# A decoder step on one core: where the rows' factors are spread, and how far the gating unit's loads stand ahead of their readers

## The chip, the core and the metric

The kernel runs on one core of one Trainium2 chip. The core has a matrix engine (PE; its weight loads are listed apart as PEld), a vector engine (DVE), a scalar engine for functions and copies (ACT), a general engine (POOL) and a sequencer that mostly issues transfers (SP). Each engine has its own queue and works through it in order; what an engine reads from another is guarded by semaphores. The metric is the device time of one execution in microseconds (us), smaller is better. One execution is also profiled; its times are read from the span's start.

## What is computed

The reference is one step of a decoder layer for a prompt (1024 rows of width 1024) and for eight sample rows that attend to a paged cache of 8192 positions. Cut to what matters here:

```python
def mixer_inputs(xn, w_in, b_f, g_sgu_v):          # xn = rmsnorm(x, g_mix)
    h = xn @ w_in                                  # columns: q | k | v | f | u | z
    q, k, v = ...
    logf = log_sigmoid(h[f] + b_f)
    u = gelu(h[u]);  z = rmsnorm(gelu(h[z]), g_sgu_v)

def sgu_prompt(u, z, w_s, b_s):                    # the gating unit, chunks of 128 rows
    mixed = einsum('hts,bcshd->bcthd', tril(w_s), z in chunks) + b_s
    return u * mixed

xp = xp + concat(rmsnorm(attention(q, k, v, logf)), rmsnorm(sgu_prompt(u, z))) @ w_o
xp = xp + cross_attend(rmsnorm(xp), memory)        # 4 heads, 256 memory tokens
xp = xp + conv_ffn(rmsnorm(xp))                    # width 2816, causal convolution of width 3
```

The sample rows pass through the same layer, with their keys and values gathered from the cache. RMSNorm of the input is not applied to x before the projection: the kernel multiplies the gain into x, multiplies by the weights, and applies each row's factor (one over the root mean square) when it takes the product out.

## The kernel before, in words

**Products.** Every float product with a weight is made of three matmuls on operands split in a high and a low part (`wh`/`wl` for weights, `xh`/`xl` for activations): high by high, high by low, low by high. Weights come in as `wr` (four buffers), ACT makes the high part (line 213) and DVE or POOL the low part (line 214), in four `wl` and five `wh` buffers. Large activation tiles share 18 buffers with the tag `u`; 512-column scratch tiles share seven with the tag `t2` (shown as `t`). PSUM tiles for products take `ba` (four) or `bb` (two) in turn by a counter (`BK`), every third one `bb`.

**Stages of the prompt.** `p1` makes q, f/u, k, v and z. Then come `attention(0)` for the first 512 rows with `fill` mixed in (the memory's keys and values, `pmem`, and then `gating(0)`, the first unit), `attention(1)`, and for each half of 512 rows: merge, output product, cross-attention, feed-forward. `gating(1)`, the second unit, is mixed into the first half's cross-attention.

**The start of p1.** `loaded(O_Q, ...)` brings x transposed (`load_x`, lines 216 and 217 split it) and the weights of q in four groups, each with the sample rows' small products (line 260). `stats(hf)` loads 512 rows of x as rows, sums their squares on ACT (line 205), and takes the root on DVE and POOL (lines 198, 199). The same function then spreads the four column factors along the free axis: DVE writes a 128x512 tile with them on diagonals (line 342), PE multiplies it by ones (line 349), and ACT copies the result into `rrow` (line 350). Both calls of `stats` and the sample's sum (`sample_sum`, lines 272 and 274) stand ahead of the queries' products: `by_cols(0)` runs 96 matmuls of four accumulators, with the four groups of weights as the outer loop (lines 423 to 425), `mm_cols(1, ...)` another 96 (lines 248 to 250). `evac_T` takes each of the eight results out with `rrow` (line 408) and splits it (lines 213, 214).

**The gating unit.** `gating(hf)` loads the gain (`gsv`, line 592) and the mixing weights (line 594, masked by DVE in line 595), and then for two pairs of 128-row chunks loads `z` and `u` (lines 602, 603), scales z (line 605, DVE), multiplies (line 613, PE) and combines (line 623, DVE). At the end it scales by the rows' factors and stores (lines 640, 641).

**The order.** All stages are generators. A `yield d` hands over control and tells how much work was just written, in units near 1 us of matmuls. `mix(main, bg, ratio)` lets the background generator take one step whenever the sum of the main one's units times the ratio exceeds what the background has used. The same units pace the sample rows' work, which is a generator of 148 steps of cache reading (`decode`; a K step multiplies on DVE or POOL in line 1205 and sums in line 1209, a V step multiplies on PE in line 1264) and then 87 smaller steps (`sample_rest`, of which the last groups read `w_down`): one step for each 7.5 units in p1, 20 in the first attention, 15 in the second, 6.0 in the middle stages, 7.5 and 8 in the feed-forward stages, 4.0 once the cache is done. Steps that are left when the prompt has ended are written behind it.

```python
def fill():
    yield from pmem()
    yield from gating(0)
att = yield from mix(att0, fill0, 1.0)
...
sq = yield from mix(cross(xt, sq), gating(1), 0.05)
```

What is written is a priority, not yet an order: a planner walks through the program with estimated durations and puts each engine's instructions in the order in which they become ready by its estimate, earlier written ones first. Buffers of one tag are handed out in the order in which their tiles are written.

Of the kernel before, what the change touches and what calls it, by code (L numbers as in the profile page):

```python
# [80 lines left out]
def build(nc, tc, ctx, a, phases=None):  # L81
# [13 lines left out]
    def nm(s):  # L95
        cnt[0] += 1
        return f"{s}_{cnt[0]}"

    def U(shape, dt=F32):
        n = 1  # L100
        for s in shape[1:]:
            n *= s
        t = upool.tile([P, UW], dt, tag="u", bufs=NU, name=nm("u"))[:, :n]
        if len(shape) == 3:
            t = t.rearrange("p (a b) -> p a b", b=shape[2])
        return t

    def T2(n=512, dt=F32):
        return tpool.tile([P, 520], dt, tag="t2", bufs=NT, name=nm("t2"))[:, :n]

    def KV():
        return dpool.tile([P, 2048], F32, tag="kv", bufs=NKV, name=nm("kv"))

    def sm(shape, tag, bufs=2, dt=F32):
        return small.tile(shape, dt, tag=tag, bufs=bufs, name=nm(tag))
# [9 lines left out]
    def BK():  # L125
        turn_[0] += 1
        return BB() if turn_[0] % BR == BR - 1 else BA()
# [66 lines left out]
    def rstd_of(ssq, n, width, tag):  # L194

        p = ssq.shape[0]
        r = sm([P, width], tag + "r", 2)[:p]
        nc.vector.tensor_scalar(r, ssq, 1.0 / n, EPS, op0=ALU.mult, op1=ALU.add)
        nc.gpsimd.tensor_tensor(r, r, mhalf[:p, :width], op=ALU.pow)
        return r  # L200

    def ssq_into(dst, src):
        n = src.shape[-1]
        j = tpool.tile([P, 1024], BF16, tag="junk", bufs=1, name=nm("junk"))[: src.shape[0], :n]
        nc.scalar.activation(j, src, AF.Square, accum_out=dst)
# [38 lines left out]
    def gemm3(out, pairs):  # L244

        n = len(pairs)
        for i, (sh, sl, mh, ml) in enumerate(pairs):
            mmul(out, sh, mh, start=(i == 0), stop=False)  # L248
            mmul(out, sh, ml, start=False, stop=False)  # L249
            mmul(out, sl, mh, start=False, stop=(i == n - 1))  # L250
# [57 lines left out]
    def p1(early):  # L308
        rstd = const.tile([P, 8], F32, tag="rstd", name="rstd")
# [19 lines left out]
        def stats(hf):  # L329
            for q in range(2):  # L330
                xr = KV().rearrange("p (c d) -> p c d", d=D)
                t0 = hf * 4 + q * 2
                with tc.issue_after(x_in):
                    nc.sync.dma_start(xr, a["x"][t0 * P : (t0 + 2) * P, :].rearrange("(c p) d -> p c d", p=P))
                for i in range(2):
                    ssq_into(ssx[:, t0 + i : t0 + i + 1], xr[:, i, :])
            c = slice(hf * 4, hf * 4 + 4)
            r = rstd_of(ssx[:, c], D, 4, "r4")
            nc.vector.tensor_copy(rstd[:, c], r)

            dg = T2()
            nc.vector.tensor_tensor(
                dg.rearrange("p (i t) -> p i t", t=P),
                ident.unsqueeze(1).broadcast_to((P, 4, P)),
                r.unsqueeze(2).broadcast_to((P, 4, P)),
                op=ALU.mult,
            )
            ps = BK()
            mmul(ps, ones, dg, start=True, stop=True)
            nc.scalar.activation(rrow[:, hf, :], ps, AF.Copy)  # L350
# [52 lines left out]
        def evac_T(ps, hf, hp, scale, hi, lo, out=None):  # L403

            c = slice(hf * 512, hf * 512 + 512)
            rows = slice(hp * P, (hp + 1) * P)
            t, h, l = T2(), T2(512, F32R), T2(512, F32R)
            nc.vector.scalar_tensor_tensor(t, ps, scale, rrow[:, hf, :], op0=ALU.mult, op1=ALU.mult)  # L408
            split(t, h, l)
            nc.scalar.dma_start(hi[rows, c], h.bitcast(F32))  # L410
            nc.scalar.dma_start(lo[rows, c], l.bitcast(F32))
            if out is not None:
                nc.sync.dma_start(out[rows, c], t)

        def by_cols(hf, ws):

            pss = [BK() for _ in range(4)]
            c = slice(hf * 512, hf * 512 + 512)
            for k in range(8):
                wh, wl = ws[k // 2][0][:, k % 2, :], ws[k // 2][1][:, k % 2, :]  # L420
                for i in range(4):
                    cb = slice(i * P, (i + 1) * P)
                    mmul(pss[i], wh[:, cb], xh[k][:, c], start=(k == 0), stop=False)
                    mmul(pss[i], wh[:, cb], xl[k][:, c], start=False, stop=False)
                    mmul(pss[i], wl[:, cb], xh[k][:, c], start=False, stop=(k == 7))
                yield 2.6
            return pss
# [14 lines left out]
        def mm_cols(hf, hp, ws, out):  # L442
            c, cb = slice(hf * 512, hf * 512 + 512), slice(hp * P, (hp + 1) * P)
            gemm3(
                out,
                [(ws[k // 2][0][:, k % 2, cb], ws[k // 2][1][:, k % 2, cb], xh[k][:, c], xl[k][:, c]) for k in range(8)],
            )

        pss = yield from by_cols(0, ws)
        for i in range(8):  # L450
            ps = BK() if i > 3 else pss[i]
            if i > 3:
                mm_cols(1, i - 4, ws, ps)
                yield 5.2
            evac_T(ps, i // 4, i % 4, 0.125, qh_d, ql_d)

# [91 lines left out]
        for tt in range(8):  # L548
            if tt < 4:
                ps = BK()  # L550
                mm_chunk(tt, ws, ps, 0, 512)
                if tt == SD:
# [5 lines left out]
                    r = rstd_of(ssv, AW, 1, "r1")  # L558
# [12 lines left out]
                    r = rstd_of(ssv, AW, 1, "r1")  # L571
# [12 lines left out]
        r = rstd_of(ssz, AW, 8, "r8")  # L584
# [5 lines left out]
    def gating(hf):  # L590
        gsv = T2()
        nc.sync.dma_start(gsv, a["g_sgu_v"].broadcast_to((P, 512)))
        wst = U([P, 8, P])
        nc.sync.dma_start(wst, a["wsT"])
        nc.vector.tensor_tensor(wst, wst, tri.unsqueeze(1).broadcast_to((P, 8, P)), op=ALU.mult)
        us_, ssu = [], sm([P, 4], "ssu", 1)
        for pr_ in range(2):
            z = U([P, 2, 512])
            u = U([P, 2, 512])
            t0 = hf * 4 + pr_ * 2  # L600
            rows = slice(t0 * P, (t0 + 2) * P)
            nc.sync.dma_start(z, zg_d[rows, :].rearrange("(c p) d -> p c d", p=P))
            nc.sync.dma_start(u, sgu_d[rows, :].rearrange("(c p) d -> p c d", p=P))
            for i in range(2):
                nc.vector.scalar_tensor_tensor(
                    z[:, i, :], z[:, i, :], rz[:, t0 + i : t0 + i + 1], gsv, op0=ALU.mult, op1=ALU.mult
                )
            yield 1
            for q in range(2):
                ps = BK()  # L610
                for j in range(4):
                    h = q * 4 + j
                    mmul(
                        ps[:, j * P : (j + 1) * P].rearrange("p (c d) -> p c d", d=64),
                        wst[:, h, :],
                        z[:, :, h * 64 : (h + 1) * 64],
                        start=True,
                        stop=True,
                    )
                for j in range(4):  # L620
                    h = q * 4 + j
                    uh = u[:, :, h * 64 : (h + 1) * 64]
                    nc.vector.scalar_tensor_tensor(
                        uh,
                        ps[:, j * P : (j + 1) * P].rearrange("p (c d) -> p c d", d=64),
                        gp[:, B_S + h : B_S + h + 1],
                        uh,
                        op0=ALU.add,
                        op1=ALU.mult,
                    )  # L630
                yield 1
            for i in range(2):
                ssq_into(ssu[:, pr_ * 2 + i : pr_ * 2 + i + 1], u[:, i, :])
            us_.append(u)
        r = rstd_of(ssu, AW, 4, "r4")
        for pr_ in range(2):
            u = us_[pr_]
            t0 = hf * 4 + pr_ * 2
            for i in range(2):
                nc.vector.tensor_scalar(u[:, i, :], u[:, i, :], r[:, pr_ * 2 + i : pr_ * 2 + i + 1], None, op0=ALU.mult)  # L640
            nc.sync.dma_start(sgn_d[t0 * P : (t0 + 2) * P, :].rearrange("(c p) d -> p c d", p=P), u)
        yield 1
# [950 lines left out]
    def prompt():  # L1593
        def fill():
            yield from pmem()
            if not G0R:
                yield from gating(0)
# [5 lines left out]
        def early():  # L1603
            next(att0)
            next(fill0)

        yield from p1(early)
        phase[0] = "att0"
        att = yield from mix(att0, fill0, MIXR)
# [150 lines left out]
```

## Time and profile before

| | |
|---|---|
| three runs | 2012.66 us median (2010.02 to 2018.85) |
| the profiled execution | 2016.49 us, of which the span from first to last instruction is 2014.7 us |
| PE busy | 1831.1 us, 91% of the span |
| DVE busy | 1329.0 us, 66% |
| ACT busy | 699.8 us, 35% |
| POOL busy | 976.4 us, 48% |
| mean granted PE clock | 0.963 |
| moved by DMA | 533.83 MB, 265 GB/s |

A row of the timeline gives the start, the length, the engine, the line, the operation, output and inputs, the shape, the count of merged instructions, and in brackets how long the engine had been idle before it and what ended that idle time. SPq rows are transfers issued by SP. A row of the windows view gives for a stretch of time each engine's busy time with its count (PE, PEld, DVE, ACT, POOL), then the granted PE clock, the DMA share and GB/s. Matmuls overlap, so a matmul's length is larger than the distance to the next one.

### The profile page before, as it was taken

The numbers are of one execution on the slowest core, as the hardware profiler recorded it, in microseconds if no ns is written. First come the engines' busy times: TensorE is split into PE (matmuls) and PEld (weight loads), VectorE is DVE, ScalarE is ACT, GpSimd is POOL, SyncE is SP. The second block draws the span as 40 slices with busy tenths as digits, with TensorE's granted clock in tenths as the row PEclk, the third lists the DMA queues.
The fourth block names the chain that finished last, engine by engine and source line by source line (L and its number), as shares of the span: only waits on it lengthen the run. The fifth ranks groups of instructions, "written<-read, shape, count | busy, mean of one in ns | idle before, by whom it ended". The sixth has DMA issues, their size and how long they took to land.

```text
span 2014.7 us, 24057 instructions
## 1 busy us (share of the span) xinstructions
PE 1831.1 (91%) x9083; PEld 1291.1 (64%) x9083; DVE 1329.0 (66%) x1456; ACT 699.8 (35%) x1284; POOL 976.4 (48%) x543
## 2 busy tenths in 40 slices
PE   3999997959998997989889998998899999899996
PEld 1797765646676655667657676676466767567772
DVE  4757766557646799998997999967524428633232
ACT  5132234436732423422322332333324433242431
POOL 1442464323267757667657675567243344232420
PEclk9999998979998998999989999999898999999999
DMA  9566799878696888788778697978755358666665
GB/s 340 189 230 209 275 325 324 262 213 236 219 355 238 316 316 326 270 316 331 275 257 338 248 330 296 373 290 322 294 185 199 119 178 278 241 196 221 251 229 189
DMA packets 161107, 533.83 MB, mean 265 GB/s; under 512 B 21832, under 2 KB 33352, under 8 KB 128224
## 3 DMA queue, kind: packets, MB, share of 16 engines
q0 software_dynamic: 38528, 270.88, 36.2%
q1 hardware_dynamic: 113248, 244.64, 35.8%
q10 hardware_dynamic: 9216, 16.78, 2.2%
q8 instruction: 71, 1.16, 0.2%
q14 instruction: 44, 0.36, 0.0%
HBM read 504.12 MB, written 28.13 MB: 264 GB/s over the span
## 4 chain that ended last, share of the span: by engine, by line
PE 59%; DVE 19%; DMA 10%; issue 5%; POOL 3%; ACT 2%; SPq 0%; POOLq 0%; DVEq 0%; ACTq 0%
PE ba L248 10%; PE ba L250 9%; PE ba L249 9%; PE bb L248 5%; PE bb L249 5%; PE bb L250 5%; DVE kv L1205 4%; PE dv L1264 3%; DVE s L1209 3%; DMA kv<-cache_k,kidx 3%; POOL wl L214 2%; DMA wr<-w_o 2%; DVE u L214 2%; PE dv L1507 1%; DVE t L1083 1%
## 5 line engine op out<-in xcount | busy, mean ns | idle before, releaser
L214 POOL TENSOR_TENSOR wl<-wr,wh 128x1024 fp32r<-128x1024 f32 (+1 forms) x184 | 458.0, 2499 | 331.7 <-PE ba L250 210.7
L213 ACT ACTIVATE wh<-wr 128x1024 fp32r<-128x1024 f32 (+2 forms) x220 | 228.1, 1042 | 327.5 <-PE ba L249 78.4
L1205 DVE TENSOR_TENSOR kv<-kv,d 128x2048 f32<-128x2048 f32 (+1 forms) x108 | 290.1, 2690 | 56.9 <-DMA kv<-cache_k,kidx 49.2
L1197 POOL DMA_INDIRECT kv<-cache_k,kidx x128 | 165.2, 1291 | 312.8 <-DVE s L1209 165.8
L1209 DVE TENSOR_REDUCE s<-kv 128x32 f32<-128x2048 f32 (+1 forms) x137 | 291.9, 2136 | 33.0 <-POOL kv L1205 32.0
L1258 POOL DMA_INDIRECT kv<-cache_v,kidx x128 | 179.6, 1403 | 182.4 <-PE dv L1264 69.6
L248 PE MATMUL ba<-wh,u 128*128 128x512 f32 (+1 forms) x612 | 239.8, 394 | 10.8 <-ACT u L213 6.3
L248 PE MATMUL ba<-u,wh 128*128 128x512 f32 x616 | 247.7, 403 | 0.0
L250 PE MATMUL ba<-u,wl 128*128 128x512 f32 x616 | 244.9, 398 | 0.0
L249 PE MATMUL ba<-u,wh 128*128 128x512 f32 x616 | 244.2, 397 | 0.0
L249 PE MATMUL ba<-wl,u 128*128 128x512 f32 (+1 forms) x612 | 236.9, 388 | 6.8 <-DVE wl L214 5.3
L250 PE MATMUL ba<-wh,u 128*128 128x512 f32 (+1 forms) x612 | 235.4, 387 | 6.8 <-DVE u L214 6.8
L1205 POOL TENSOR_TENSOR kv<-kv,d 128x2048 f32<-128x2048 f32 (+1 forms) x29 | 121.8, 4205 | 86.1 <-DMA kv<-cache_k,kidx 74.0
L1264 PE MATMUL dv<-kv,s 128*32 128x512 f32 x1024 | 139.9, 627 | 15.5 <-DMA kv<-cache_v,kidx 14.1
L248 PEld LDWEIGHTS ba<-wh,u 128*128 128x128 f32 x612 | 118.7, 194 | 53.7 <-issue 18.0
L248 PEld LDWEIGHTS ba<-u,wh 128*128 128x128 f32 x616 | 117.1, 190 | 47.6 <-issue 15.9
L250 PEld LDWEIGHTS ba<-wh,u 128*128 128x128 f32 x612 | 118.1, 193 | 40.0 <-DVE u L214 9.3
L249 PEld LDWEIGHTS ba<-wl,u 128*128 128x128 f32 x612 | 118.6, 194 | 36.0 <-DVE wl L214 5.9
L250 PEld LDWEIGHTS ba<-u,wl 128*128 128x128 f32 x616 | 116.6, 189 | 33.3 <-issue 7.3
L249 PEld LDWEIGHTS ba<-u,wh 128*128 128x128 f32 x616 | 116.9, 190 | 32.6 <-issue 6.8
L248 PE MATMUL bb<-u,wh 128*128 128x512 f32 x312 | 125.6, 402 | 2.1 <-DVE t L408 2.1
L249 PE MATMUL bb<-u,wh 128*128 128x512 f32 x312 | 124.2, 398 | 0.0
(409 smaller groups left out, 3049.4 us busy)
## 6 DMA issues: line engine op xcount, KB each, us to landing
wr<-w_up SPq DMA_DIRECT2D x88, 512.0 KB
kv<-w_up SPq DMA_DIRECT2D x22, 1024.0 KB
wr<-w_down SPq DMA_DIRECT2D x40, 512.0 KB
kv<-w_down SPq DMA_DIRECT2D x11, 1024.0 KB
wr<-w_in SPq DMA_DIRECT2D x16, 512.0 KB
wr<-w_o SPq DMA_DIRECT2D x16, 512.0 KB
wr<-w_cq SPq DMA_DIRECT2D x16, 512.0 KB
wr<-w_co SPq DMA_DIRECT2D x16, 512.0 KB
```

The lines of the kernel that those rows point to most:

```text
L213: nc.scalar.activation(h, src, AF.Copy)
L214: (eng or nc.vector).tensor_tensor(l, src, h.bitcast(F32), op=ALU.subtract)
L248: mmul(out, sh, mh, start=(i == 0), stop=False)
L249: mmul(out, sh, ml, start=False, stop=False)
L250: mmul(out, sl, mh, start=False, stop=(i == n - 1))
L1083: nc.vector.scalar_tensor_tensor(hc[:, 1:], pv[:, :511], cw[1], hc[:, 1:], op0=ALU.mult, op1=ALU.add)
L1197: nc.gpsimd.indirect_dma_start(kv, None, a["cache_k"], off(kidx[:, b, ch : ch + 1]))
L1205: eng.tensor_tensor(kvv[:, i : i + m, :], kvv[:, i : i + m, :], qb.unsqueeze(1).broadcast_to((P, m, 512)), op=ALU.mult)
L1209: nc.vector.tensor_reduce(s[:, ch * 4 + i : ch * 4 + i + m, :].rearrange("p k h -> p (k h)"), kvv[:, i : i + m, :].rearrange("p k (h d) -> ...
L1258: nc.gpsimd.indirect_dma_start(kv, None, a["cache_v"], off(kidx[:, b, ch : ch + 1]))
L1264: mmul(dv[32 * j : 32 * j + 32, :], s[:, ch * 4 : ch * 4 + 4, :].rearrange("p k h -> p (k h)"), kvv[:, j, :], start=(ch == 0), stop=(ch == ...
L1507: mmul(ps[32 * j : 32 * j + 32, q * 256 : (q + 1) * 256].rearrange("p (f c) -> p f c", f=2), xsT[:, k, :], rv[:, k], start=(k < 4), stop=( ...
```

## The change

```diff
@@ stats(hf), in p1
             r = rstd_of(ssx[:, c], D, 4, "r4")
             nc.vector.tensor_copy(rstd[:, c], r)

+        def row_factors(hf):
+
+            r = rstd[:, hf * 4 : hf * 4 + 4]
             dg = T2()
             nc.vector.tensor_tensor(
                 dg.rearrange("p (i t) -> p i t", t=P),
                 ident..., r..., op=ALU.mult,
             )
             ps = BK()
             mmul(ps, ones, dg, start=True, stop=True)
             nc.scalar.activation(rrow[:, hf, :], ps, AF.Copy)
@@ the queries, in p1
         pss = yield from by_cols(0, ws)
+        row_factors(0)
         for i in range(8):
             ps = BK() if i > 3 else pss[i]
             if i > 3:
                 mm_cols(1, i - 4, ws, ps)
+                if i == 4:
+                    row_factors(1)
                 yield 5.2
             evac_T(ps, i // 4, i % 4, 0.125, qh_d, ql_d)
@@ gating(hf)
             nc.sync.dma_start(z, ...)
             nc.sync.dma_start(u, ...)
+            yield 6
             for i in range(2):
                 nc.vector.scalar_tensor_tensor(z[:, i, :], z[:, i, :], rz..., gsv, ...)
-            yield 1
+            yield 3
             for q in range(2):
                 ps = BK()
```

The second half of `stats` becomes a function of its own, `row_factors`, that reads the factors from the kept tile `rstd` instead of the small tile they were computed in. It is called for the first half behind the 96 matmuls of `by_cols(0)`, and for the second half behind the first 24 of the other 96. In the gating unit control is handed over between the loads of a pair and the scaling of z, with 6 units, and the units behind the scaling are 3 instead of 1. A unit of gating that had 7 units in all now has 23. No operation is added or taken away.

## The prediction

> **What bounds the kernel now.** I read the page first, then PE's idle time through the slices, the chain of waits, and the timeline at the places the change touches.
>
> ```profile
> span 2014.7 us, 24057 instructions
> ...
> PE   3999997959998997989889998998899999899996
> ...
> PE 59%; DVE 19%; DMA 10%; issue 5%; POOL 3%; ACT 2%; SPq 0%; POOLq 0%; DVEq 0%; ACTq 0%
> ```
>
> The first row of digits is PE's busy share by slices of about 50 us: nearly always 8 or 9, so PE carries the kernel, and the chain that ends last is PE for 59%. What can be won lies where PE stands still. The largest such place is the first slice, with a 3; slice nine, near 400 us, has another gap.
>
> ```profile
> 8.50 1.22 DVE L214 TENSOR_TENSOR wl<-wr,wh 128x1024 fp32r<-128x1024 f32 x1 [0.20 <-ACT wh L213]
> ...
> 10.14 1.92 PE L260 MATMUL ba<-wr,xsT 128*32 128x512 f32 x4 [0.69 <-DMA wr<-w_in]
> ...
> 18.87 1.92 PE L260 MATMUL ba<-wr,xsT 128*32 128x512 f32 x4 [1.18 <-DMA wr<-w_in]
> ...
> 21.40 1.42 DVE L217 SCALAR_TENSOR_TENSOR u<-wr,gp,u 128x512 fp32r<-128x512 f32 x2 [0.23 <-ACT u L216]
> ...
> 38.24 0.68 DVE L342 TENSOR_TENSOR t<-cp,r4r 128x512 f32<-128x512 f32 x1
> ...
> 38.98 2.07 PE L349 MATMUL bb<-t,ones 128*128 128x512 f32 x2 [18.19 <-DVE t L342]
> ...
> 41.28 0.63 PE L424 MATMUL bb<-u,wh 128*128 128x512 f32 x1
> ...
> 41.71 0.53 PE L425 MATMUL bb<-u,wl 128*128 128x512 f32 x1
> ...
> 47.84 1.02 PE L349 MATMUL ba<-t,ones 128*128 128x512 f32 x2
> ...
> 48.79 1.02 PE L274 MATMUL ba<-t,cp 128*8 128x512 f32 x2
> ...
> 49.75 0.51 PE L423 MATMUL ba<-u,wh 128*128 128x512 f32 x1
> ```
>
> In this timeline PE waits 18.19 us for the diagonal tile of line 342, which itself needs row sums of x. The queries' products need none of that: their last operands for the first half are ready at 22.82 (21.40 + 1.42), the first at 9.72 (8.50 + 1.22). They stand behind line 349 because of the PSUM tiles: at first they write `bb` alone, and those for `ba` begin at 49.75, right behind the second line 349 and line 274, which were written earlier and take `ba` first.
>
> **The change part by part.** (1) *The spreading products.* Two `ba`/`bb` tiles, two DVE, two PE and two ACT operations move; none is added. Ahead of `by_cols(0)` only the sample's sum is left, on a `bb` tile, so three of the four accumulators can start with the first weights.
>
> ```profile
> 22.80:39.00 16.20, 0.02 (x1) 0.02 (x1) 5.10 (x10) 10.85 (x18) 3.57 (x4) 1.00 1.01 391
> ...
> 64.00:85.40 21.40, 21.40 (x94) 17.45 (x93) 15.02 (x14) 3.68 (x5) 10.98 (x6) 1.00 0.65 231
> ```
>
> ```profile
> 84.94 0.25 PE ba L250
> ```
>
> The first row (windows) shows 16.2 us without PE work; the second 94 matmuls in 21.40 us, 0.228 each; the third (chain) the end of the queries at 85.19. The least the change does is to let the products start at 22.82 instead of 39: 16.2 us. The most, if they also fill PE from 9.72: three groups of line 260 (3 x 1.92 = 5.8), 192 matmuls (43.8), line 274 (1.02), two line 349 (2 x 1.02) and some 2 us at the slow distance of 0.43 seen at 41.28 to 41.71, end at 64.4, which is 20.8 earlier. I take 19, between these, since the rows of line 260 leave PE free more than half the time. The tile of line 342 is ready at 38.92 and PE comes to it near 41, so it is no longer waited for; what is late next are the takings-out.
>
> ```profile
> 68.13 0.68 DVE L408 SCALAR_TENSOR_TENSOR t<-bb,u 128x512 f32<-128x512 f32 x1
> ...
> 101.63 0.68 DVE L408 SCALAR_TENSOR_TENSOR t<-ba,u 128x512 f32<-128x512 f32 x1
> ```
>
> Eight of these, first and last shown, run 33.5 us, 4.8 from one to the next; a query product takes 24 x 0.228 = 5.5. So they keep up if they begin near 42, and the next weights' products move up with the rest. Everything up to the first attention is paced by PE, so I let the 19 us stand to the end. If the takings-out cannot begin earlier, it is nothing (a rival below).
>
> In p1's new order the matmuls come in bursts between loads. Those before 22.82 have 13.1 - 5.8 = 7.3 us of PE time; at 0.43 that is 17 matmuls in place of 32, 15 x 0.228 = 3.4 us lost, so this term would be 15.6 and the sum below 3.4 higher. The Trainium skill (TensorE: Matmul & The Clock Gate, section "HAM oscillation — how this bites in real kernels") says that bursts shorter than their waits let the PE clock fall back each time, which speaks against part of this gain; the slow distance at 41.28, after 16 us of idling, agrees with it.
>
> (2) *The first gating unit.*
>
> ```profile
> 404.25 0.35 SPq L592 DMA_DIRECT2D t<-g_sgu_v  x1
> ...
> 405.16 0.38 SPq L602 DMA_DIRECT2D u<-zg_d  x1
> ...
> 410.20 1.22 DVE L595 TENSOR_TENSOR u<-u,cp 128x1024 f32<-128x1024 f32 x1 [5.09 <-DMA u<-wsT]
> ...
> 411.76 1.42 DVE L605 SCALAR_TENSOR_TENSOR u<-u,rz,t 128x512 f32<-128x512 f32 x2 [0.33 <-DMA u<-zg_d]
> 413.23 2.07 PE L613 MATMUL bb<-u,u 128*128 128x128 f32 x8 [6.99 <-DVE u L605]
> ...
> 419.36 0.36 SPq L602 DMA_DIRECT2D u<-zg_d  x1
> ...
> 428.05 1.42 DVE L605 SCALAR_TENSOR_TENSOR u<-u,rz,t 128x512 f32<-128x512 f32 x2 [8.82 <-DMA u<-zg_d]
> 429.51 2.08 PE L613 MATMUL ba<-u,u 128*128 128x128 f32 x8 [8.64 <-DVE u L605]
> ...
> 664.59 1.05 PE L613 MATMUL bb<-u,u 128*128 128x128 f32 x8
> ```
>
> ```profile
> SPq L592 <- DMA o_mv<-t: 11.5, 1, 11.5
> ```
>
> PE stands still 6.99 + 8.64 = 15.6 us, and its four groups of eight then take about 2.07 each, 1.05 in the second unit at 664.59: 4 x 1.02 = 4.1 more. The loads cannot go out earlier: the last row shows SP waiting 11.5 us for a scratch buffer. What changes is the distance of the readers. Adding up the units of both generators, before, the loads and the first products both follow step 24 of the attention's 32; now the scaling follows step 27 and the products step 29. The second pair's loads follow step 30 and its products come behind the last step. So attention work that was queued behind line 613 on PE (scores, transposes, values) runs in the gap. But line 595 is written with the loads, and DVE still waits 5.09 us at it, later 8.82 at line 605, if the planner puts them where it thinks the data there; the attention's maxima queue behind them on DVE, and four `ba` tiles of scores are all that PE can run ahead. The ends are 0 and 15.6 + 4.1 = 19.7. I take 9, a little under half.
>
> (3) *The second unit.* The cross-attention has 123.3 units (norm 4.1, queries 8 x 5.2, heads 36, output 8 x 5.2), times 0.05 is 6.17. The loads' 6 units use this up, so all but the first pair's loads now comes behind its last output product, in one block ahead of the feed-forward's norm.
>
> ```profile
> 688.96 0.43 SPq L602 DMA_DIRECT2D u<-zg_d  x1
> ...
> 707.15 1.40 DVE L605 SCALAR_TENSOR_TENSOR u<-u,rz,t 128x512 f32<-128x512 f32 x2
> ...
> 765.58 1.11 DVE L623 SCALAR_TENSOR_TENSOR u<-ba,gp,u 128x128 f32<-128x128 f32 x4
> ...
> 786.75 7.38 DVE L1205 TENSOR_TENSOR kv<-kv,d 128x2048 f32<-128x2048 f32 x1
> ...
> 792.52 1.94 PE L1264 MATMUL dv<-kv,s 128*32 128x512 f32 x8 [7.48 <-DMA kv<-cache_v,kidx]
> ```
>
> ```profile
> 784.00:807.10 23.10, 11.07 (x58) 6.25 (x57) 21.47 (x22) 7.30 (x15) 18.24 (x12) 0.70 0.88 313
> ```
>
> Before, nothing waited here: 18 us lay between the loads at 688.96 and their scaling. The block would stand in the stretch 784 to 807.1, where PE is idle 12 us but DVE is busy 21.47 of 23.10. PE's 32 small matmuls (4 x 1.05 = 4.2) go into that idle time. DVE gets 4 x 1.11 + 2 x 1.40 = 7.2 us in front of the norm's scalings, and if the second pair's loads go out only there, up to the 8.64 seen in part 2. SP issues ahead of the program where `u` buffers are free, so this is less likely. The ends are -4.2 and +15.8; I take +5.
>
> (4) *The sample's pace.* Sixteen more units in each gating unit are 16/20 + 16/6.0 = 3.5 cache steps earlier, and with one step per 4 units at the end, six more of the small steps before the prompt ends: two left behind it instead of eight.
>
> ```profile
> 1984.00:2003.20 19.20, 13.51 (x62) 2.88 (x52) 1.90 (x5) 0.76 (x3) 0.54 (x1) 0.91 0.82 306
> ```
>
> ```profile
> PE dv L1546 <- DMA kv<-w_down: 5.6, 3, 2.3
> ```
>
> PE's work for them is the same in either place; gone can be what PE waits there, 19.20 - 13.51 = 5.7 us, nearly all for `w_down`. Ends 0 and -5.7; I take -3.
>
> Sum: -19 - 9 + 5 - 3 = -26. The profiled execution took 2016.49, so 1990.5 against it; it lies 3.8 above the median of 2012.66, so I predict 1987 for the median.
>
> **The rivals.** *The start gives its gain back.* Taking out needs `t2` buffers, DVE and ACT, and the next stage's low parts queue behind it on DVE; if it still ends near 102, the next products start no earlier. For it: the last takings-out come 17 us behind the last query product. Against: DVE is busy only 15.02 of 21.40. Then -9 + 5 - 3 = -7, a median of 2006. *The waits stay with the first unit* (the change then does not do what it says): DVE stops at lines 595 and 605 as now, and PE behind it. For it: both DVE waits are for data and no load moves forward. Against: PE has scores and values ready. Then -19 + 5 - 3 = -17, 1996. *Slower:* three sample steps more are written around the block of part 3; if each makes DVE stand at its K tile (7.38) and PE at its V tile (7.48) in turn ahead of the feed-forward's norm, that is 3 x 14.9 = 44.6, with DVE's 7.2 it is 51.8, against gains of 31: 2012.66 + 20.8 = 2033. It decides from 31 us at this place. For it: DMA is at 0.88 there, and PE already waits once. Against: steps done there are not done later.
>
> **How the numbers follow.** A measurement of this kernel cannot tell less than about 0.5%, 10 us, from no change. My forecast gets 0.60; the start's gain lost 0.12; the first unit's waits kept 0.15; the slower case 0.07; 0.06 is for more gain than the forecast's own range, 1968 to 2000. Its ends are near the terms' bounds: -21 - 20 - 4 - 6 is 1962, and -16 - 2 + 8 - 0 is 2003. The range with the rivals is 1968 to 2007; it leaves out the slower case and the ends. Faster by over 0.5% (below 2002.6): 0.60 + 0.15 + 0.06 = 0.81; within: 0.12; slower: 0.07.
>
> **What would show it.** Right: the first query product before 25 us, no wait for line 342 above 2 us, queries ended by 70; waits of line 613 for line 605 well under 15.6 in sum; line 613's last groups behind the cross-attention's last product; fewer `w_down` groups behind the prompt. Wrong: query products still one accumulator at a time; the first attention as long as before; the stretch from the last output product to the feed-forward's first product above 40 us instead of 23; or a new order of the planner's far from these places that costs PE time, for which no row here gives a price.

## The result, and the profile after

| | median | runs | profiled execution | span |
|---|---|---|---|---|
| before | 2013.69 us | 20 (2001.65 to 2026.03) | 2016.49 us | 2014.7 us |
| after | 1989.51 us | 20 (1970.94 to 2016.55) | 1995.11 us | 1993.3 us |

The ratio of the two is 0.9859, 95% interval 0.9832 to 0.9886: 28 us faster. It leaves out two slow runs of the changed kernel (2003.60 and 2016.55, over 1.5% above its fastest), so it gives more than the 24 us between the medians. A second comparison (after_again, below) gave 0.9898, 0.9867 to 0.9929, some 21 us. Predicted was 1987.

The page of the changed kernel (span; PE's busy share in 40 slices; shares of the chain that ended last):

```profile
span 1993.3 us, 24049 instructions
...
PE   7599996959999789899999998989898999999998
...
PE 55%; DVE 13%; DMA 6%; issue 4%; POOL 3%; ACT 1%; POOLq 0%; DVEq 0%; SPq 0%; ACTq 0%
```

The first slice is a 7 where it was a 3, but the second is a 5 where it was a 9. The last is an 8 where it was a 6. (The changed kernel's lines stand 3 later in `row_factors`, 7 later from gating on.) The start, in its timeline:

```profile
9.14 0.80 PE L426 MATMUL ba<-u,wh 128*128 128x512 f32 x1
...
47.53 0.69 DVE L411 SCALAR_TENSOR_TENSOR t<-ba,u 128x512 f32<-128x512 f32 x1 [2.62 <-ACT u L353]
...
52.25 0.79 PE L248 MATMUL bb<-u,wh 128*128 128x512 f32 x1 [9.02 <-DVE t L411]
...
55.38 1.00 SPq L1176 DMA_DIRECT2D d<-qs_d  x2
...
59.05 2.29 DVE L1212 TENSOR_TENSOR kv<-kv,d 128x2048 f32<-128x2048 f32 x1 [6.86 <-DMA d<-qs_d]
...
59.07 11.53 POOL L1212 TENSOR_TENSOR kv<-kv,d 128x2048 f32<-128x2048 f32 x2 [13.14 <-DMA d<-qs_d]
...
61.26 4.98 DVE L214 TENSOR_TENSOR t<-t,t 128x512 fp32r<-128x512 f32 x1
66.17 5.51 DVE L1186 TENSOR_TENSOR_SCAN d<-rmask,d 128x512 f32<-128x512 f32 x1
...
77.17 0.68 DVE L345 TENSOR_TENSOR t<-cp,rstd 128x512 f32<-128x512 f32 x1
...
77.99 2.04 PE L352 MATMUL ba<-t,ones 128*128 128x512 f32 x2 [17.25 <-DVE t L345]
...
91.66 0.40 PE L250 MATMUL ba<-u,wl 128*128 128x512 f32 x1
```

The first query product stands at 9.14 instead of 40, and the first taking-out at 47.53 instead of 68.13. But PE waits 9.02 us for a taking-out (52.25), and the second spreading product waits 17.25 us for its diagonal tile. DVE makes that tile at 77.17, behind a K step of the sample (L1212), which first waits 6.86 us for `qs_d` and then runs beside the K steps of GpSimd; the splitting (L214) and the scan (L1186) behind it take 4.98 and 5.51 us. The last query product ends at 92, later than the 85.19 of before. The windows of the changed kernel show what it costs PE; before, it was busy for 24.00 of 24.00 in both:

```profile
40.00:64.00 24.00, 11.72 (x37) 8.35 (x35) 8.56 (x9) 6.89 (x10) 8.36 (x5) 0.79 0.81 318
64.00:88.00 24.00, 10.01 (x34) 7.42 (x35) 23.97 (x12) 2.90 (x4) 15.77 (x7) 0.64 0.55 187
```

The first gating unit, from the changed kernel's timeline:

```profile
410.57 1.08 POOL L1204 DMA_INDIRECT kv<-cache_k,kidx  x1 [10.49 <-PE dv L1271]
411.94 1.42 POOL L1265 DMA_INDIRECT kv<-cache_v,kidx  x1 [0.30 <-issue]
...
414.24 1.00 POOL L1204 DMA_INDIRECT kv<-cache_k,kidx  x1 [0.30 <-DVE mT L1239]
...
419.61 9.23 SPq L608 DMA_DIRECT2D u<-zg_d  x1
...
438.24 1.41 DVE L612 SCALAR_TENSOR_TENSOR u<-u,rz,t 128x512 f32<-128x512 f32 x2 [10.72 <-DMA u<-zg_d]
439.70 2.08 PE L620 MATMUL ba<-u,u 128*128 128x128 f32 x8 [14.76 <-DVE u L612]
```

The first pair no longer makes PE wait for its scaling, the second one does, for 14.76 us: before, the two waits were 6.99 and 8.64. The load of the second pair is issued at 419.61, as before (419.36), but the issue alone takes SP 9.23 us instead of 0.36; three gatherings of the sample's cache were issued shortly ahead of it. The second unit and the feed-forward's first product:

```profile
786.59 0.61 PE L620 MATMUL bb<-u,u 128*128 128x128 f32 x4
...
788.67 1.95 PE L620 MATMUL ba<-u,u 128*128 128x128 f32 x16
790.46 1.06 PE L620 MATMUL bb<-u,u 128*128 128x128 f32 x8
...
796.93 1.11 DVE L630 SCALAR_TENSOR_TENSOR u<-bb,gp,u 128x128 f32<-128x128 f32 x4
...
798.76 0.69 PE L958 MATMUL ba<-cp,u 128*128 128x128 f32 x2 [6.25 <-DVE u L949]
...
813.16 0.78 PE L248 MATMUL bb<-u,wh 128*128 128x512 f32 x1
```

It stands in one block behind the cross-attention's last output product (begun at 786.37, the row ahead of the block), and the norm's transposes wait 6.25 us: 26.8 us from that product to the feed-forward's first, 23.4 before. The end, before and after (last rows of the prompt's output on DVE, of the sample's on ACT):

```profile
1986.01 1.42 DVE L1132 SCALAR_TENSOR_TENSOR u<-u,rn3r,u 128x512 f32<-128x512 f32 x2 [0.65 <-POOL rn3r L199]
...
2003.16 0.60 ACT L1557 ACTIVATE d<-dv 128x512 f32<-128x512 f32 x1 [18.18 <-PE ms L1546]
```

```profile
1982.25 1.42 DVE L1139 SCALAR_TENSOR_TENSOR u<-u,rn3r,u 128x512 f32<-128x512 f32 x2 [0.66 <-POOL rn3r L199]
...
1981.63 0.60 ACT L1564 ACTIVATE d<-dv 128x512 f32<-128x512 f32 x1 [0.41 <-PE ms L1553]
```

The prompt ends only 3.8 us earlier; what is gone is the sample's tail behind it, 17 us before and nothing now.

### The profile page after: what moved, and what is told of

Same layout as the page of the kernel before. It is cut to its first block, busy times and chain, and to the rows that moved or that the text cites. A ratio compares the mean times of both kernels' runs of the same rounds, so it can differ in the third digit from the quotient of the medians.

```text
span 1993.3 us, 24049 instructions
## 1 busy us (share of the span) xinstructions
PE 1825.0 (92%) x9083; PEld 1286.7 (65%) x9083; DVE 1319.4 (66%) x1457; ACT 696.7 (35%) x1282; POOL 985.4 (49%) x544
## 4 chain that ended last, share of the span: by engine, by line
PE 55%; DVE 13%; DMA 6%; issue 4%; POOL 3%; ACT 1%; POOLq 0%; DVEq 0%; SPq 0%; ACTq 0%
PE ba L248 9%; PE ba L249 9%; PE ba L250 9%; PE bb L248 5%; PE bb L249 4%; PE bb L250 4%; PE dv L1271 4%; DVE kv L1212 3%; DVE s L1216 3%; POOL wl L214 2%; DMA kv<-cache_k,kidx 2%; DMA kv<-cache_v,kidx 1%; PE dv L1514 1%; DMA u<-zg_d 1%; PE ba L1043 1%
## 5 line engine op out<-in xcount | busy, mean ns | idle before, releaser
L214 POOL TENSOR_TENSOR wl<-wr,wh 128x1024 fp32r<-128x1024 f32 (+1 forms) x184 | 465.3, 2541 | 329.6 <-PE ba L250 218.8
L1212 DVE TENSOR_TENSOR kv<-kv,d 128x2048 f32<-128x2048 f32 (+1 forms) x108 | 297.9, 2762 | 66.0 <-DMA kv<-cache_k,kidx 59.1
L1265 POOL DMA_INDIRECT kv<-cache_v,kidx x128 | 175.4, 1371 | 210.4 <-PE dv L1271 99.1
L1212 POOL TENSOR_TENSOR kv<-kv,d 128x2048 f32<-128x2048 f32 (+1 forms) x30 | 124.7, 4166 | 100.0 <-DMA kv<-cache_k,kidx 83.2
L248 PEld LDWEIGHTS ba<-wh,u 128*128 128x128 f32 x620 | 117.9, 190 | 42.1 <-issue 17.5
L248 PEld LDWEIGHTS ba<-u,wh 128*128 128x128 f32 x608 | 116.0, 191 | 43.3 <-issue 15.6
L248 PE MATMUL bb<-u,wh 128*128 128x512 f32 x320 | 130.2, 407 | 11.2 <-DVE t L411 11.2
L249 PEld LDWEIGHTS ba<-u,wh 128*128 128x128 f32 x608 | 116.0, 191 | 36.7 <-issue 11.9
L249 PE MATMUL bb<-u,wh 128*128 128x512 f32 x320 | 128.7, 402 | 0.0
```

The costliest lines, as they stand in the source:

```text
L214: (eng or nc.vector).tensor_tensor(l, src, h.bitcast(F32), op=ALU.subtract)
L1212: eng.tensor_tensor(kvv[:, i : i + m, :], kvv[:, i : i + m, :], qb.unsqueeze(1).broadcast_to((P, m, 512)), op=ALU.mult)
L1265: nc.gpsimd.indirect_dma_start(kv, None, a["cache_v"], off(kidx[:, b, ch : ch + 1]))
```

## The experiments

My first theory (T) took that last picture at its word: the gain is the sample's pace, and the two moves give nothing. The rival (R) was the prediction's own first term.

**1. The parts, one at a time.** start_only is before with the p1 part of the change, gating_only before with the two yields 6 and 3. pace_only changes one number of before:

```diff
@@ gating(hf), its last line
-        yield 1
+        yield 17
```

after_old_pace is the changed kernel, with gating's new units not counted for the sample:

```diff
+class Silent(float):
+    pace = 0.0
+class Paced(float):
+    pace = 1.0
@@ gating(hf)
-            yield 6
+            yield Silent(6)
-            yield 3
+            yield Paced(3)
@@ the loop over prompt()
-        acc[0] += t
+        acc[0] += getattr(t, "pace", t)
```

> The kernel before with only the p1 part of the change: the spreading products behind the queries' first products, gating untouched. Theory T (the gain of the change is made by the sample's pace; the start is paid back at the second spreading product): the first query product moves from 40 to about 9 us, but a wait of about 17 us for the second diagonal tile of line 345 appears near 61 us, the prompt is 4 us earlier at most, and the whole is 0 to 6 us faster. Rival R (the prediction's term 1: the start's gain stands to the end): 15 to 21 us faster.

> The kernel before with only the two yields of gating (6 behind the loads, 3 behind the scaling); p1 as before. T: 15 to 22 us faster, the sample's work 18 to 40 us earlier from the first half's merge on, and its last w_down products no longer behind the prompt's last ones; the waits of the product at line 613 in the first unit stay near 15 us in sum. R: 0 to 8 us faster.

> The kernel before with one number changed: the last yield of gating gives 17 units in place of 1, so that each unit adds the same 16 units to the sample's pace as the change does, while no reader and no load of the gating unit moves. T: 12 to 22 us faster, as the change itself. R: 0 to 5 us faster. If it is the distance of the readers that pays: 0 to 3 us here, with gating_only at 9 or more.

> The changed kernel, with the 6 and 3 units of gating counted in the interleaving of gating with the attention as in the change, but not for the sample's pace (it counts 0 and 1 there, as before). All moves stay; only the sample's steps stand where they stood. T: 0 to 6 us faster than before, with the sample's tail behind the prompt again. R: 15 us faster or more.

Ratios to before: start_only 0.9991 (0.9972 to 1.0010), gating_only 0.9994 (0.9973 to 1.0016), pace_only 0.9977 (0.9957 to 0.9998), after_old_pace 0.9907 (0.9885 to 0.9929). T falls: the pace alone gives 5 us, and the changed kernel without its pace still gains 19. R falls too: the start alone gives 2. The table shows where each kernel stands against before, in one profile each. Its heads are the starts of the same instructions in before (us): the fifth F tile's gelu, attention ahead of the gating unit, attention behind it, its last output, the first half's first, 22nd and last step of the feed-forward (the residual's sum for the last), the prompt's last output, the sample's last copy.

| kernel | 127 | 403 | 469 | 552 | 827 | 1018 | 1279 | 1987 | 2003 |
|---|---|---|---|---|---|---|---|---|---|
| start_only | -4.6 | -6.8 | -6.7 | -5.0 | -8.8 | -9.3 | -8.9 | -7.4 | -7.3 |
| gating_old_pace | -3.6 | -5.8 | -14.7 | -11.9 | +3.5 | -7.3 | -13.9 | -13.2 | -12.0 |
| after_old_pace | -5.0 | -10.1 | -21.8 | -18.8 | -7.9 | -18.8 | -22.8 | -21.0 | -20.9 |
| pace_only | -1.1 | -3.7 | -2.6 | +10.3 | +23.2 | +17.5 | +10.6 | +14.6 | -3.2 |
| gating_only | -3.4 | -3.8 | -7.5 | +4.7 | +7.8 | +11.2 | +11.6 | +16.4 | -1.4 |
| after | -3.5 | -1.0 | -3.9 | +8.0 | +8.1 | -10.3 | -5.0 | -3.8 | -21.5 |
| after_again | -3.1 | -2.3 | -6.2 | +4.3 | +11.6 | -11.8 | -5.5 | -2.4 | -20.2 |
| both_early | -1.6 | +2.1 | -2.8 | +8.1 | +2.6 | -14.3 | -12.2 | -6.3 | -24.1 |
| start_late | -18.8 | -11.0 | -10.4 | -2.1 | +1.4 | -7.7 | -12.1 | -4.3 | +0.1 |
| after_late | -17.0 | -7.2 | -0.9 | +0.6 | +5.5 | -11.7 | -14.4 | -11.4 | -29.2 |
| both_early_old_pace | -3.8 | 0.0 | -7.4 | -4.4 | +6.5 | -4.8 | -9.0 | -5.3 | -4.4 |
| after_old_pace_late | -18.1 | -9.6 | -9.7 | -5.4 | +5.3 | -5.8 | -15.7 | -7.5 | -2.1 |
| gating_ffn0_745 | -4.0 | -2.0 | -5.5 | +6.2 | +11.6 | +11.6 | +10.3 | +13.0 | -4.8 |

Four kernels with p1 unchanged (gating_old_pace, pace_only, gating_only and gating_ffn0_745 of part 4) stand at -1.1 to -4.0 in the first column: so much do two profiles differ there by themselves. pace_only shows what the pace does: the prompt ends 14.6 us later, since it carries the sample's work, the tail of 17 is gone, and 3 remain.

**2. The gating unit, and the start without its wait.** gating_old_pace is gating_only with the classes above. both_early calls the second spreading product right behind the first:

```diff
         row_factors(0)
+        row_factors(1)
@@
-                if i == 4:
-                    row_factors(1)
```

after_again is the changed kernel beside them, both_early_old_pace both_early with the classes.

> The kernel before with only the gating part, p1 as before, and the 6 and 3 units not counted for the sample's pace. Theory T2 (the distance of the readers pays in the first gating unit, and gating_only lost it because its sample steps, pushed ahead, put three cache gatherings in front of the second zg_d load): the second pair's first product waits under 4 us for its scaling in place of 14, the first attention is 9 to 13 us shorter, and the whole is 9 to 16 us faster than before. Rival (the gain needs both parts at once, by a chance of the planner's order): 0 to 5 us faster.

> The changed kernel with both spreading products issued right behind the first half's query products, so that the second diagonal tile stands on VectorE ahead of the takings-out and of the sample's K step. If the 17 us wait at the second spreading product is what took the start's gain: the wait is gone, and the whole is 8 to 14 us faster than the changed kernel (13.9 is what term 1 still owes: 19 less the 5 that came). If VectorE's queue itself is late there (takings-out and K step behind a load of the sample's queries): the wait goes over to the takings-out, and the time is that of the changed kernel within 4 us.

> The changed kernel again, on the same chip as the others of this group, to compare it with after_old_pace by their ratios to the kernel before: 0.984 to 0.988. If the sample's pace pays about 3 us in it, as term 4 said, it is 0 to 8 us below after_old_pace.

> both_early with the 6 and 3 units not counted for the sample's pace. If the first gating unit is freed by the old pace and the start by the earlier tile, the two add: 30 to 40 us faster than before. If the sample's tail behind the prompt counts in full: about as after_old_pace, 18 to 22 us faster.

gating_old_pace: 0.9946 (0.9925 to 0.9967), 11 us. From its waits, and from those and the timeline of gating_only:

```profile
PE ba L622 <- DVE u L614: 4.2, 2, 2.4
```

```profile
PE ba L614 <- DVE u L606: 13.9, 1, 13.9
...
416.69 8.89 SPq L602 DMA_DIRECT2D u<-zg_d  x1
```

The two have the same moves and differ in the pace alone. With the old pace PE's waits in the unit fall from the 15.6 of before to 4.2, and the table has 8.9 us more behind the unit than ahead of it. With the new pace a sample step's gatherings stand ahead of the second load, whose issue takes 8.89 us, and the wait stays. So it is shown that the new pace brings the wait back. That the gatherings make the issue long, as T2 has it, is not. The five kernels with three gatherings in the 9 us ahead of this load issue it in 8.72 to 9.28 us, after_late with two (and a third just ahead) in 5.00, all those with none in 0.36 to 0.37. But the kernel before issued the second unit's load at 688.96 in 0.43 us behind four gatherings; two of them:

```profile
686.33 0.94 POOL L1197 DMA_INDIRECT kv<-cache_k,kidx  x1 [0.30 <-DVE cr L1020]
687.57 0.95 POOL L1258 DMA_INDIRECT kv<-cache_v,kidx  x1 [0.31 <-issue]
```

What else a long issue takes stays open. As both_early_old_pace then gained only 5 us (0.9975, 0.9959 to 0.9992; 18 to 40 were expected) although its waits for the scaling are as short, 2.8, a short wait there is not enough.

both_early: 0.9904 (0.9883 to 0.9925), after_again 0.9898 (0.9867 to 0.9929), a shade short of the 0.984 to 0.988 expected: no difference between the two. after_again lies 2 us below after_old_pace, and the intervals can tell that neither from nothing nor from the 8 us expected at most. both_early's waits of PE:

```profile
PE ba L248 <- DVE t L411: 12.2, 3, 7.6
PE ba L260 <- DVE t L411: 10.8, 1, 10.8
PE ba L352 <- DVE t L345: 2.2, 1, 2.2
```

The wait for the diagonal tile fell from 17.3 to 2.2 and went over to the takings-out (23.0, where the changed kernel had 9.0), which stand behind the same K step on DVE.

**3. The sample's first K steps out of the way.** In start_late, after_late and after_old_pace_late the sample begins behind the queries and then catches up:

```diff
         acc[0] += t
+        units[0] += t
+        n = 0
         while bgs and not hold[0] and acc[0] >= PACE[phase[1] or phase[0]]:
+            if phase[0] == "p1" and (units[0] < 42 or n):
+                break
+            n += 1
```

> start_only, and in p1 the sample's steps begin only behind the queries (after 42 units), then at most one per unit step until they have caught up; nothing else moves. If the sample's first K step in front of the takings-out on VectorE is what took the start's gain: no wait above 5 us at the second spreading product or at the takings-out, the Z product and the first attention 15 to 19 us earlier than in the kernel before, and the whole 12 to 20 us faster than before. If the K step only stood in for something else that is late there: the first attention 4 to 8 us earlier, as in start_only, and 0 to 6 us in all.

> The changed kernel with the same late beginning of the sample's steps. If the K step is what took the start's gain: the first attention 10 to 15 us earlier than in the changed kernel; in all 24 to 40 us faster than before, if the gain passes the first gating unit (its wait of 14 us at the second pair stays, since the pace is the change's). Otherwise within 5 us of the changed kernel.

> after_old_pace with the same late beginning of the sample's steps: start without the K step, gating unit without the three gatherings ahead of its second load. If the terms add, 18.7 (after_old_pace) and 10 to 14 more: 28 to 34 us faster than before, which would be below both kernels. If the gain of the start is lost on the way (the sample's debt is paid in K and V at the price that was saved): 16 to 22 us.

start_late 1.0023 (1.0003 to 1.0043), after_late 0.9841 (0.9810 to 0.9872), after_old_pace_late 1.0005 (0.9983 to 1.0028). From start_late's timeline:

```profile
42.92 1.02 PE L352 MATMUL ba<-t,ones 128*128 128x512 f32 x2
...
59.89 1.02 PE L352 MATMUL ba<-t,ones 128*128 128x512 f32 x2
...
310.73 0.69 ACT L586 ACTIVATE t<-bb,rstd 128x512 f32<-128x512 f32 x1 [16.58 <-DMA u<-ql_d]
...
313.92 0.47 PE L762 MATMUL bb<-cp,t 128*128 128x128 f32 x1 [16.26 <-ACT t L744]
```

Neither spreading product waits any more, and the table has the F tile 18.8 us earlier, of which 1 to 4 lie within what two profiles differ by. So the sample's early steps, of which a K step stands in DVE's queue, were what held the start up, and the start is worth some 15 to 18 us where it is made. One wait was not theirs: PE still waits 8.52 us for a taking-out at 52.46, where the expectation had none above 5. The gain does not last: 11.0 us are left ahead of the gating unit, where PE has waited 16.26 us for ACT (5.28 at the same place before) and ACT 16.58 us for transfers, and 2.1 at the attention's end. In all start_late is 5 us slower than before. The first reading's "12 to 20 in all" is wrong, and after_old_pace_late gains nothing, where 16 to 34 us were expected. after_late gains 32 us, within its 24 to 40, though it stands only 6 and 7 us ahead of the changed kernel at 403 and 552 (10 to 15 were expected). It is the fastest kernel measured, but its interval overlaps that of the changed kernel.

**4. The first feed-forward.** Up to 827 gating_only and the changed kernel stand alike (+7.8 and +8.1), at 1018 21 us apart. Both programs have the same stage there (DVE gets 47 and 48 of the K multiplies); their order on each engine differs. DVE's groups that read two SBUF tiles, from 830 to 1280, in gating_only and in the changed kernel:

```profile
L1206 DVE TENSOR_TENSOR kv<-kv,d 128x2048 f32<-128x2048 f32 x47 | 157.5, 3352 | 23.3 <-DMA kv<-cache_k,kidx 23.3
...
L1092 DVE TENSOR_TENSOR t<-t,t 128x512 f32<-128x512 f32 x22 | 40.7, 1852 | 0.3
L214 DVE TENSOR_TENSOR u<-t,u 128x512 fp32r<-128x512 f32 x22 | 24.4, 1110 | 0.7 <-ACT u L213 0.7
```

```profile
L1212 DVE TENSOR_TENSOR kv<-kv,d 128x2048 f32<-128x2048 f32 x48 | 147.3, 3070 | 26.9 <-DMA kv<-cache_k,kidx 26.9
...
L214 DVE TENSOR_TENSOR u<-t,u 128x512 fp32r<-128x512 f32 x22 | 26.8, 1217 | 0.7 <-ACT u L213 0.7
...
L1098 DVE TENSOR_TENSOR t<-t,t 128x512 f32<-128x512 f32 x22 | 21.1, 958 | 0.5
```

Nearly the same work takes 222.6 us in the one and 195.2 in the other. The difference lies wholly ahead of the 22nd step: up to there (834.5 to 1029.4 and 834.9 to 1007.9) the groups take 105.5 and 74.1 us, from there on 114.5 and 115.1. gating_ffn0_745 gives that stretch another order:

```diff
-PACE = {..., 'ffn0': 7.5, ...}
+PACE = {..., 'ffn0': 7.45, ...}
```

> gating_only with one number changed: in the first half's feed-forward a sample step per 7.45 units in place of 7.5, so that its 47 steps each stand a little earlier, by a third of a step at its end, and the planner orders that stretch anew; everything ahead of it is the same. Theory: 20 us between gating_only and the changed kernel hang on the order within this stretch alone, in which VectorE is busy for 97% and its products of two SBUF tiles (K multiply, line 1092, line 214) take 0.7 us or 5, as they fall beside GpSimd's splits or not: the sum of these three groups from 830 to 1280, 222.6 us in gating_only and 195.2 in the changed kernel, moves by 5 us or more, and the end of the stretch moves the same way by two thirds of it. Rival (the order within the stretch does not matter, the 20 us come with the start's 4 us): the end of the stretch within 3 us of gating_only, the whole within 5 us.

0.9984 (0.9958 to 1.0010); the same groups:

```profile
L1206 DVE TENSOR_TENSOR kv<-kv,d 128x2048 f32<-128x2048 f32 x47 | 166.2, 3537 | 10.5 <-DMA kv<-cache_k,kidx 10.5
L1092 DVE TENSOR_TENSOR t<-t,t 128x512 f32<-128x512 f32 x22 | 35.2, 1601 | 0.3
L214 DVE TENSOR_TENSOR u<-t,u 128x512 fp32r<-128x512 f32 x22 | 22.0, 999 | 0.1
```

The sum is 223.4, as in gating_only, and the stretch ends at +10.3 instead of +11.6. By what was written down this is the rival's outcome: the end within 3 us of gating_only, the whole within 5. It decides little: apart from one step that changes its place near 890, the order differs from gating_only's only behind 1055, and the 21 us fall ahead of that. That DVE's slower products cost these 21 us is argued from rows, not shown by an experiment. For it speaks that over the profiles of all fourteen kernels the stretch from the first to the 22nd step lasts 168 to 195 us and grows with the sum of the three groups in it, 68 to 106 us (correlation 0.92). Nor is it shown why the new p1 part brings the better order with it, though the four kernels that have it with the new pace (after, after_again, both_early, after_late) all drop by 17 to 23 us from 827 to 1018, and those with the new pace but without it by 6 (pace_only) and not at all (gating_only, gating_ffn0_745).

## Why the prediction was right in sum and wrong in its terms

The time, 1989.5 (and by the second comparison 1994), lies in the range and near 1987. The working does not hold up as well.

- **Term 1 (the start, -19).** The first query product and the three accumulators at once came as said; the first taking-out came at 47.53 instead of near 42. Of the signs named, the wait for the diagonal tile is 17.25 us where it was to be under 2, and the queries end at 92 and not by 70. The failing steps are "they keep up if they begin near 42" and "I let the 19 us stand to the end". I had counted DVE's free time, 15.02 busy of 21.40, and not what stands in its queue: a K step whose operand comes late, and products that take 5 us beside GpSimd's. Alone, the start gave 1.8 us by the ratio, 7 in the profile. This is the rival "The start gives its gain back", nearly at its price, by another cause than the `t2` buffers; start_late shows that even 15 to 18 us, made without the K step, are lost before the attention ends.
- **Term 2 (the first gating unit, -9).** As a move it was sized right: 15.6 us of waits became 4.2, 8.9 us in the table (gating_old_pace). In the changed kernel it failed, and the rival "The waits stay with the first unit" came true: 14.76 remain. I had the rule for the sample's pace in term 4 and did not ask which step it would push into this place.
- **Term 3 (the second unit, +5).** The block stands where I put it. The stretch grew by 3.4 us in the changed kernel; with the old pace the table loses more than that from 552 to 827 (15.4 in gating_old_pace), but the feed-forward gives all of it back by 1279. Sample steps explain that in part: in gating_old_pace DVE and GpSimd do 31 K multiplies from 552 to 827 instead of 28, and 44 instead of 47 in the feed-forward. In the table nothing of the term is left at 1279.
- **Term 4 (the pace, -3).** pace_only gave 4.6 us by the ratio (0.4 to 8.7), 3.0 in the profile, and its reason held: PE's work is the same in either place. The sight of a tail that is gone is no gain of 17.
- **The sum.** The parts alone make 1.8 + 10.9 + 4.6 = 17 us, against 28 and 21 measured. They do not add in pairs either: gating with its pace gave 1, both_early_old_pace 5, after_old_pace 19. What I named at the end as having no price, a new order far from the edits, is the nearest account of that: combinations miss their expected gains by up to some 20 us (after_old_pace_late), and the changed kernel gains 18 us between 827 and 1018, where no term of mine stands. Terms 1 and 2 failed and that gain stood in for them. That the sum came near 1987 is luck. What makes the gain in the first feed-forward stays open.
- **The slower rival.** The stretch it spoke of took 26.8 us, far from the 31 more that it needed.
- **The clock.** In the prediction I took some 2 us for the slow distance, and feared more of it in the bursts before 22.82. There it did not come: 46 query products stand before 22.82, where 32 or 17 were reckoned, most of them 0.23 apart, and the granted clock is 1.00. It came behind the long waits. From 40 to 88 the granted clock is 0.79 and 0.64 in the changed kernel, where before it was 1.00 in both windows. The Trainium skill (TensorE: Matmul & The Clock Gate, section "HAM oscillation — how this bites in real kernels"), which has bursts between long waits run cold, agrees with these rows.

## What to carry to other kernels

When a wait is taken from the head of a chain, read the queue of each engine behind it for work of other streams, with its operands' arrival, and not the engine's free share. A number that paces two things moves both: give the distance of the readers and the pace of the background work separate numbers, and test them separately. Here parts that look independent differed by 1% in combination: a planner ordered them anew, and VectorE was busy for 96% of a later stage (827 to 1018 in the kernel before). So the combination has to be measured.

## What the hardware showed beside that

A product of two SBUF tiles on DVE that takes 0.69 us took 4.98 beside GpSimd's K product, and the scan 5.51 (61.26 and 66.17 above; the same scan took 1.22 in start_late). In the kernel before, line 1091's product took at most 0.76 us in the 33 cases with no product of GpSimd (a K product or a weight's splitting) beside it, and 2.82 in the median of the ten with one. The taking-out, which reads PSUM, stayed at 0.66 to 0.69 (0.68 at 100.38 in the changed kernel, beside a K product of GpSimd), and the K step's reduction stayed near 2.28. The Trainium skill (SBUF — State Buffer, section "Who interferes with whom") says that a DVE instruction with two SBUF inputs contends with a GpSimd instruction that reads SBUF, and that the later one blocks; these rows agree. At 98.18 in the changed kernel it was the other way round: DVE's K product took its usual 2.28 us, and GpSimd's, begun at 97.86, took 7.08 instead of the 4.91 of the one before it. The effect speaks against term 1, and I had not weighed it.

The issue of one load took 9.23 us instead of 0.36 with three gatherings issued shortly before it on GpSimd's queue, and it held up all that SP had behind it. Gatherings alone do not do it: 0.43 us at 688.96 in the kernel before, behind four of them.
